# Values and output gate of the input projection as eight pairs of tiles with seven part products, x loaded tile by tile, key rotation on GpSimd

## The chip, the cores and the metric

The kernel runs on one core of one Trainium2 chip. The metric is the device time of one execution in microseconds (us), the lower the better. The core's engines are named as the profile names them: PE (TensorE: matmuls, with PEld for the loads of its stationary operand), DVE (VectorE), ACT (ScalarE), POOL (GpSimd) and SP (SyncE, whose queue issues the DMAs).

## The reference

The reference is one layer of a bidirectional encoder over 2048 rows of 1024 columns. Its first step is the subject here: an RMS norm and one large product, whose columns are cut up and go to different consumers.

```python
xn = rms_norm(h, ln_mix_g)
proj = xn @ w_in                      # 2512 columns: q, k, v, o of 512 each; 16 gates; 256 cq; 128 ckv; 64 kr
y_a = mlstm_group(q, k, v, o, gates + b_gates, conv_qk_w, conv_qk_b, mlstm_norm_g)
y_b = mla_group(cq, ckv, kr, q_norm_g, w_uq, kv_norm_g, w_ukv, cos, sin)
h = h + concat(y_a, y_b) @ w_out
h = h + conv_gated_mlp(rms_norm(h), ...)
h = h + sigmoid(rms_norm(h) @ w_ple_gate) * rms_norm(p @ w_ple_proj)
out = rms_norm(h)
```

`v` goes into the mLSTM as it is; `o` goes through a sigmoid and multiplies the mLSTM's normed output. `cq` and `ckv` are normed, `kr` is rotated by its position (`x1*cos - x2*sin`, `x2*cos + x1*sin`, 32 columns each).

## The kernel before

**Number format.** A float32 product is made from three matmuls in the PE's faster fp32r format: each operand is split into a rounded part and a remainder (`split`, lines 116 to 123: ACT casts at line 120, DVE subtracts at line 123), and `mm3` (lines 131 to 136) adds low x high, high x low and high x high. `split_g` (125 to 129) does the same for weights scaled by the norm's gain (ACT 128, DVE 129). The norm's inverse root is applied to the product's rows afterwards.

**The input projection, `in_proj` from line 176**, works in four stages. x comes already transposed, as eight k steps of 128 columns. One row tile is 128 of the 2048 rows; there are 16.

1. The "rest" columns (gates, cq, ckv, kr: 464). For each row tile `load_x` (221) loads x, `split_x` (242) puts its two parts into buffers that hold all of x from then on, and `nat` (212) runs 24 matmuls (8 k steps of 3). `ssq_x` (228 to 240) squares x on ACT, adds on DVE, sums over partitions with a matmul against ones (line 237), and takes the power -1/2 on POOL (240) into one column of `rcol`. The epilogue `rest` (248 to 276) adds the gate bias on DVE (252), copies the scaled product on ACT (255), takes the two norms' squares on ACT (261, 262) and their inverse roots on POOL (263, then `rsq`, 141 and 143), scales on DVE (265, 266), and rotates kr with six DVE instructions of 32 columns and a copy (269 to 275). `turn_rest` (278 to 284) transposes the 512 columns with four PE transposes (281), copies on ACT (283) and writes `rest_d`. The loop runs the epilogue two tiles behind the loads, the transposes two further behind.
2. The values: `load_w` loads and splits 512 columns of weights, `nat` makes the 16 tiles, DVE scales, and the result goes to `v_d`. Steps of the gate computation (`gates`, 631) are put between.
3. The output gate: the same, with a sigmoid on ACT and a multiplication by the norm's gain on DVE, to `o_d`.
4. q and k transposed, column tile by column tile (`block`, `conv`, lines 379 to 456), with x as the moving operand out of the buffers that hold all of it. Here `pump` (373) puts pieces of side work between the blocks (`absorb` at 518 and `q_up` at 563, products of the attention weights): a counter gains 0.986 a call and one piece runs for each whole unit. Here PE's order is fixed as written; in the stages before it a scheduler orders the instructions of each engine by data dependence and its own estimates.

After this come the mLSTM, the attention, the output projection and the feed-forward part (`stream`). The feed-forward part already computes pairs of row tiles with seven products in place of eight: `prep_a` (1367) and `prep_b` (1398) form the sums of a pair's x blocks and split them (through `up_pair`, 1350), and the weights' sums have the names of the table `OPX` (1167).

Eviction and accumulation use PSUM banks from four pools: four banks of the pool `sc` (`bank`), two of `tr` (`tbank`), one for the attention's products and one for small things (`pml`).

Of the kernel before, what the change touches and what calls it, by code (L numbers as in the profile page):

```python
# [36 lines left out]
LAG_T, LAG_X, LAG_R = 1, 2, 2  # L37
# [5 lines left out]
def pause(n):  # L43

    for _ in range(n):
        yield
# [14 lines left out]
class Block:  # L61
# [114 lines left out]
    def in_proj(self):  # L176
        nc, d = self.nc, self.d
        xh = [[self.at(f"x{4 * c + 2 * f}", [P, 4, 512], F32R, f"xh{c}{f}") for f in range(2)] for c in range(4)]
        xl = [[self.at(f"x{4 * c + 2 * f + 1}", [P, 4, 512], F32R, f"xl{c}{f}") for f in range(2)] for c in range(4)]
        wrot, rrot, trot, srot = _rot("w", (*range(9), 13)), _rot("w", range(9, 13)), _rot("t", range(4)), _rot("s", range(3))  # L180
        w_in = d["w_in"][0].rearrange("(a b p) c -> a p b c", b=2, p=P)

        def load_w(c0, n, before=None):

            out, raws = [], []

            def load(k2, parts=1):
                raw = self.at(next(rrot), [P, 2, 512], name="wraw")
                for i in range(parts):
                    bs = slice(2 * i // parts, 2 * (i + 1) // parts)  # L190
                    nc.sync.dma_start(raw[:, bs, :n], w_in[k2, :, bs, c0:c0 + n])
                raws.append(raw)
                return raw

            if before:
                load(0, 2)
                before(0)
                load(1, 2)
                before(1)
                load(2)  # L200
                load(3)
            for k2 in range(KT // 2):
                if k2 == len(raws):
                    load(k2)
                raw = raws[k2]
                for b in range(2):
                    w = self.at(next(wrot), [P, 2, 512], F32R, "wsp")
                    self.split_g(raw[:, b, :n], gcol[:, 2 * k2 + b:2 * k2 + b + 1], w[:, 0, :n], w[:, 1, :n])
                    out.append(w)
            return out  # L210

        def nat(st, ws, n):
            ps = self.bank()
            c, o = st // 4, (st % 4) * P
            for kt in range(KT):
                f, k = divmod(kt, 4)
                self.mm3(ps[:, :n], xh[c][f][:, k, o:o + P], xl[c][f][:, k, o:o + P],
                         ws[kt][:, 0, :n], ws[kt][:, 1, :n], kt == 0, kt == KT - 1)
            return ps

        def load_x(st):

            t = self.at(next(rrot) if st else "u2", [P, KT, P], name="x_t")
            if st:
                nc.sync.dma_start(t, d["x_turned"][:, :, st * P:(st + 1) * P])
            return t

        def ssq_x(st, x_t):

            sq = self.at("w13", [P, KT, P], name="x_sq")  # L230
            nc.scalar.activation(sq, x_t, AF.Square)
            ss = self.at("t7", [P, 4, P], name="x_ss")
            nc.vector.tensor_tensor(ss, sq[:, 0:4], sq[:, 4:8], op=ALU.add)
            nc.vector.tensor_tensor(ss[:, 0:2], ss[:, 0:2], ss[:, 2:4], op=ALU.add)
            ps = self.pml.tile([P, 4], F32, name="ssp", tag="ml")
            for i in range(2):
                nc.tensor.matmul(ps, ss[:, i], ones, start=i == 0, stop=i == 1)
            t = self.stat(1, "rsm")
            nc.vector.tensor_scalar(t, ps[:, 0:1], 1.0 / D, EPS, op0=ALU.mult, op1=ALU.add)
            nc.gpsimd.tensor_tensor(rcol[:, st:st + 1], t, self.nhalf[:, :1], op=ALU.pow)  # L240

        def split_x(st, x_t):
            c, o = st // 4, (st % 4) * P
            for f in range(2):
                self.split(x_t[:, 4 * f:4 * f + 4], xh[c][f][:, :, o:o + P], xl[c][f][:, :, o:o + P])


        def rest(st):
            ps = nat(st, ws, NREST)
# [8 lines left out]
            cos, sin, tt = sc[:, 0], sc[:, 1], sc[:, 2:6]  # L258
# [9 lines left out]
            x1, x2 = rs[:, 384:416], rs[:, 416:448]  # L268
            nc.vector.tensor_tensor(tt[:, 0, :], x1, cos, op=ALU.mult)
# [5 lines left out]
            nc.vector.tensor_copy(nn[:, 448:512], nn[:, 384:448])  # L275
# [11 lines left out]
        nc.sync.dma_start(gcol, d["g_turned"])  # L287
# [3 lines left out]
        nq, xq = {}, {}  # L291

        xq[0] = load_x(0)

        def first(f):

            fs = slice(4 * f, 4 * f + 4)
            if f < 2:
                nc.sync.dma_start(xq[0][:, fs], d["x_turned"][:, fs, 0:P])
                self.split(xq[0][:, fs], xh[0][f][:, :, 0:P], xl[0][f][:, :, 0:P])  # L300

        ws = load_w(OFF_R, NREST, first)
        for st in range(NT + LAG_X):
            if st + 1 < NT:
                xq[st + 1] = load_x(st + 1)
            if st == 0:
                gn = self.at("t5", [P, 384], name="gn")
                self.row_bcast(gn[:, 0:256], d["q_norm_g"][0], 256)
                self.row_bcast(gn[:, 256:384], d["kv_norm_g"][0], 128)
                bg = self.row_bcast(self.cst.tile([P, 16], F32, name="bg"), d["b_gates"][0], 16)  # L310
            if 1 <= st < NT:
                split_x(st, xq[st])
            if 0 <= st - 1 < NT:
                ssq_x(st - 1, xq.pop(st - 1))
            if 0 <= st - LAG_X < NT:
                nq[st - LAG_X] = rest(st - LAG_X)
            if 0 <= st - LAG_X - LAG_R < NT:
                turn_rest(st - LAG_X - LAG_R, nq.pop(st - LAG_X - LAG_R))

        nc.sync.dma_start(self.r_d.rearrange("(t p) -> p t", p=P), rcol)  # L320
        gates = self.gates()

        ws = load_w(OFF_V, 512)
        for st in range(NT):
            ps = nat(st, ws, 512)
            if st < LAG_R:
                turn_rest(NT - LAG_R + st, nq.pop(NT - LAG_R + st))
            t = self.at(next(trot), [P, 512], name="vo")
            nc.vector.tensor_scalar(t, ps, rcol[:, st:st + 1], None, op0=ALU.mult)
            nc.sync.dma_start(self.v_d[st], t)  # L330
            if st >= LAG_R:
                next(gates, None)
# [10 lines left out]
        for _ in gates:  # L343
            pass
# [1700 lines left out]
```

## Time and profile before

| what | us |
|---|---|
| median of 3 runs | 2892.84 (2892.28 to 2895.26) |
| the profiled execution | 2900.96 |
| its span on the core | 2899.2 |
| PE busy | 2853.5 |
| DVE busy | 2041.1 |
| ACT busy | 1524.4 |
| POOL busy | 158.0 |
| first matmul of the rest stage starts | 7.69 |
| first matmul of the values starts | 106.72 |
| values and output gate end | 283.92 |

A page of the profile gives an engine's busy time as a share of the span. Durations of single instructions overlap by their pipeline's length on PE, so a matmul's cost is read from the distance of starts, not from its own length. In a group's row, the number after the second bar is the idle time of that engine before the group and the instruction that ended it. A window's row gives busy time by engine (PE, PEld, DVE, ACT, POOL), then the granted PE clock as a share of full speed, the DMA share and GB/s.

### The profile page before, as it was taken

How to read it: one execution, taken by the hardware profiler on the slowest of the kernel's cores; microseconds unless marked ns; L12 is line 12 of the kernel's file. 1: busy time of each engine (PE TensorE's matmuls, PEld its weight loads, DVE VectorE, ACT ScalarE, POOL GpSimd, SP SyncE). 2: the span in 40 equal slices, each digit the busy share in tenths (PEclk: the TensorE clock that was granted, in tenths of full speed). 3: DMA queues.
4: the chain of work that ended last, by engine and by line, in shares of the span. 5: the costliest groups of instructions: out<-in, count | busy, mean ns of one | idle time of the engine just before them, and what ended most of it. 6: DMA issues, size and time to landing. Idle time of an engine off the chain costs nothing.

```text
span 2899.2 us, 40167 instructions
## 1 busy us (share of the span) xinstructions
PE 2853.5 (98%) x14110; PEld 2390.1 (82%) x14110; DVE 2041.1 (70%) x3790; ACT 1524.4 (53%) x3014; POOL 158.0 (5%) x295
## 2 busy tenths in 40 slices
PE   8999999999999999999999999999999999999998
PEld 7888888888888888788788888788888788888787
DVE  7521555777777777876677877767777867576787
ACT  7311544556666566765755555655555423254765
POOL 3100000000000010001000000000000000002111
PEclk9999999999999999999999999999999999999999
DMA  6612545653333333478834554657776757476865
GB/s 194 127 59 76 162 122 165 218 160 118 107 111 97 97 116 110 129 240 266 266 139 170 188 178 141 212 179 232 231 240 207 243 176 263 158 260 213 274 214 163
DMA packets 408314, 508.94 MB, mean 176 GB/s; under 512 B 34080, under 2 KB 271664, under 8 KB 408112
## 3 DMA queue, kind: packets, MB, share of 16 engines
q1 hardware_dynamic: 408112, 506.37, 55.3%
q8 instruction: 111, 1.82, 0.3%
q14 instruction: 91, 0.75, 0.1%
HBM read 324.16 MB, written 182.12 MB: 175 GB/s over the span
## 4 chain that ended last, share of the span: by engine, by line
PE 84%; DMA 5%; DVE 5%; ACT 3%; issue 3%; POOL 1%; SPq 0%; ACTq 0%; POOLq 0%; DVEq 0%
PE fy L1435 21%; PE fz L1435 14%; PE fx L1435 14%; PE bk L133 13%; PE ppv L989 3%; PE tb L977 3%; PE bk L914 2%; PE bk L916 2%; PE bk L915 2%; PE bk L918 2%; PE bk L917 2%; PE fs L133 2%; PE ppv L990 2%; PE gb L133 1%; PE mb L852 1%
## 5 line engine op out<-in xcount | busy, mean ns | idle before, releaser
L1435 PE MATMUL fz<-op,fw 128*128 128x512 f32 x1968 | 477.1, 391 | 2.7 <-ACT fw L120 2.7
L1435 PE MATMUL fy<-op,fw 128*128 128x512 f32 x1968 | 478.1, 391 | 1.6 <-ACT fy L1547 1.6
L1435 PE MATMUL fx<-op,fw 128*128 128x512 f32 x1968 | 476.0, 390 | 0.0
L1435 PEld LDWEIGHTS fy<-op,fw 128*128 128x128 f32 x1968 | 370.4, 189 | 79.4 <-ACT fy L1547 2.4
L1435 PEld LDWEIGHTS fz<-op,fw 128*128 128x128 f32 x1968 | 367.5, 188 | 79.5 <-ACT fw L120 3.6
L1435 PEld LDWEIGHTS fx<-op,fw 128*128 128x128 f32 x1968 | 368.0, 188 | 76.2 <-ACT fy L1547 0.2
L1435 PE MATMUL fy<-op,fwd 128*128 128x512 f32 (+1 forms) x984 | 239.8, 392 | 2.8 <-DVE uv L1420 2.6
L120 ACT CAST pt<-tb 128x512 fp32r<-128x512 f32 x256 | 147.2, 587 | 171.2 <-PE tb L977 170.4
L133 PE MATMUL bk<-wsp,xh 128*128 128x512 f32 (+1 forms) x768 | 234.1, 386 | 0.0
L1435 PEld LDWEIGHTS fy<-op,fwd 128*128 128x128 f32 x984 | 183.7, 189 | 41.7 <-DVE uv L1420 3.7
L919 DVE TENSOR_REDUCE mx<-bk 128x1 f32<-128x512 f32 x256 | 174.7, 684 | 40.5 <-PE bk L918 39.3
L123 DVE TENSOR_TENSOR pt<-tb,pt 128x512 fp32r<-128x512 f32 x256 | 174.1, 684 | 30.7 <-ACT pt L120 28.9
L937 ACT ACTIVATE pe<-bk,nm 128x512 f32<-128x512 f32 x256 | 174.8, 696 | 38.2 <-DVE nm L931 33.5
L989 PE MATMUL ppv<-pt,kv 128*128 128x512 f32 x512 | 188.6, 406 | 0.5 <-DVE pt L123 0.5
L133 PEld LDWEIGHTS bk<-wsp,xh 128*128 128x128 f32 x768 | 145.2, 189 | 25.1
L133 PE MATMUL bk<-wsp,xl 128*128 128x512 f32 (+1 forms) x384 | 150.7, 392 | 7.7 <-DVE xl L123 7.7
L133 PE MATMUL bk<-xh,wqk 128*128 128x512 f32 x480 | 157.1, 393 | 0.0
L977 PE MATMUL tb<-ident,pe 128*128 128x128 f32 x1024 | 150.3, 273 | 4.4 <-DVE pt L123 3.8
L990 PE MATMUL ppv<-pt,kv 128*128 128x256 f32 x512 | 144.7, 283 | 0.0
L977 PEld LDWEIGHTS tb<-ident,pe 128*128 128x128 f32 x1024 | 121.8, 140 | 25.0 <-DVE pt L123 6.8
L120 ACT CAST fw<-hraw 128x1024 fp32r<-128x1024 f32 (+1 forms) x72 | 70.2, 980 | 116.4 <-PE fx L1435 58.9
L123 DVE TENSOR_TENSOR fw<-fwr,fw 128x1024 fp32r<-128x1024 f32 x88 | 107.4, 1220 | 26.9 <-ACT fw L120 26.9
(363 smaller groups left out, 5113.5 us busy)
## 6 DMA issues: line engine op xcount, KB each, us to landing
fwr<-in_w_up SPq DMA_DIRECT2D x66, 512.0 KB, 5.2
fh<-h_d SPq DMA_DIRECT2D x48, 512.0 KB, 4.2
h_d<-fh SPq DMA_DIRECT2D x48, 512.0 KB, 4.0
s_d<-fwr SPq DMA_DIRECT2D x44, 512.0 KB, 3.3
fws<-s_d SPq DMA_DIRECT2D x44, 512.0 KB, 3.7
rw<-row_d SPq DMA_DIRECT2D x32, 512.0 KB, 5.5
tw_d<-tsum SPq DMA_DIRECT2D x60, 256.0 KB, 5.4
opr<-tw_d SPq DMA_DIRECT2D x60, 256.0 KB, 4.7
```

The lines of the kernel that those rows point to most:

```text
L120: nc.scalar.copy(hi, src)
L123: (sub or nc.vector).tensor_tensor(lo, src, _f(hi), op=ALU.subtract)
L133: mm = lambda *a, **k: self.nc.tensor.matmul(*a, **k, skip_group_check=more)
L914: mm(ps, ql, kh[:, ks], start=True, stop=False)
L915: mm(ps, qr, self.krl[:, ks], start=False, stop=False)
L916: mm(ps, qh, kl[:, ks], start=False, stop=False)
L919: nc.vector.tensor_reduce(s.mx[:, kb:kb + 1], ps, axis=AX.X, op=ALU.max)
L937: nc.scalar.activation(s.pe[:, kb % 2], s.banks[kb], AF.Exp, bias=s.nm, scale=ASCALE, accum_out=s.rs[:, kb:kb + 1])
L977: nc.tensor.transpose(t[:, j, :], s.p[kb][:, j * P:(j + 1) * P], self.ident)
L989: mm(w.ps, vh[:, ks], pts[kb][:, j], start=kt == 0, stop=False, skip_group_check=True)
L990: mm(w.ps[:, 0], vl[:, ks], pts[kb][:, j, 0], start=False, stop=kt == NT - 1, skip_group_check=True)
L1435: nc.tensor.matmul(out, a[:, k * P:(k + 1) * P], parts[lo][:, cols], start=first, stop=lo == 1 and k == last, skip_group_check=more)
```

## The change

The rest stage and the two stages after it are rewritten; lines of the new kernel are meant in this section.

- **First block.** The first four row tiles are made together, k step by k step, in four banks (`first_block`): each k step loads 512 rows of x and a piece of weights, splits both and runs 12 matmuls. Eight 128-column matmuls of the identity precede it. The sum of squares of the four tiles is formed along the way, and one instruction each makes four inverse norms.
- **x tile by tile.** Tiles 4 to 15 are loaded and split one at a time into buffers that are used again, and no copy of all x is kept. x is loaded again for the pairs (`load_pair`) and a third time for q and k (`load_qx`, 16 loads of 512 KB with 16 splits).
- **Key rotation on GpSimd.** The seven DVE instructions become five on GpSimd: two multiplications of 64 columns, a subtraction and an addition of 32, a copy of 64.
- **Values and gate in pairs.** With the values' weights as the left and the gate's as the right half of the columns, and the upper and lower half of the k steps, each pair of row tiles is a 2 x 2 block product made of seven products of 12 matmuls. The weight sums (`vo_sums`, `vo_late`) are made during the rest stage and the first pair, the sums of x by `prep_a` and `prep_b`. Two products of each pair (`rest_y`, `rest_z`) run in the next pair, those of the last pair in the q/k stage. Pairs 0 and 1 begin with one more matmul, which opens the bank that `nc.scalar.copy(s.y, x)` then fills.
- **Inverse norms.** `rcol` is turned by a PE transpose and written to `r_d` as 16 rows of 128, not element by element.
- **Around it.** The transposes of the last tiles move behind the pairs' preparation; the q/k stage's first column takes its four blocks in the order 0, 3, 1, 2; the side work's counter starts at -11 and gains 1.12 a call, and two pauses in `absorb` change (5 to 3; 2 to 3 for three of four heads).

The core of the diff:

```diff
+        def inv_rms(st, parts):
+            n = len(parts)
+            ps = self.pml.tile([P, n, 4], F32, name="ssp", tag="ml")
+            for i, ops in enumerate(parts):
+                for k, p in enumerate(ops):
+                    nc.tensor.matmul(ps[:, i], p, ones, start=k == 0, stop=k == len(ops) - 1)
+            t = self.stat(n, "rsm")
+            nc.vector.tensor_scalar(t, ps[:, :, 0], 1.0 / D, EPS, op0=ALU.mult, op1=ALU.add)
+            nc.gpsimd.tensor_tensor(rcol[:, st:st + n], t, self.nhalf[:, :n], op=ALU.pow)
...
+        def first_block():
...
+                self.split_g(raws[kt // 2][:, kt % 2, :NREST], gcol[:, kt:kt + 1], w[:, 0, :NREST], w[:, 1, :NREST])
+                self.split(xr[kt], x[:, 0], x[:, 1])
+                ws.append(w)
+                for n, (a, e) in enumerate(((0, 0), (1, 0), (0, 1))):
+                    for st in range(4):
+                        nc.tensor.matmul(ps[st][:, :NREST], x[:, a, st * P:(st + 1) * P], w[:, e, :NREST],
+                                         start=kt == 0 and n == 0, stop=kt == KT - 1 and n == 2)
+                if kt:
+                    sq = self.at(f"u{kt % 2}", [P, 512], name="x_q")
+                    nc.scalar.activation(sq, xr[kt], AF.Square)
+                    tt(acc, acc, sq, op=ALU.add)
...
-            nc.vector.tensor_tensor(tt[:, 0, :], x1, cos, op=ALU.mult)
-            nc.vector.tensor_tensor(tt[:, 1, :], x2, sin, op=ALU.mult)
-            nc.vector.tensor_tensor(tt[:, 2, :], x2, cos, op=ALU.mult)
-            nc.vector.tensor_tensor(tt[:, 3, :], x1, sin, op=ALU.mult)
-            nc.vector.tensor_tensor(nn[:, 384:416], tt[:, 0, :], tt[:, 1, :], op=ALU.subtract)
-            nc.vector.tensor_tensor(nn[:, 416:448], tt[:, 2, :], tt[:, 3, :], op=ALU.add)
-            nc.vector.tensor_copy(nn[:, 448:512], nn[:, 384:448])
+            turn, x12 = nc.gpsimd.tensor_tensor, rs[:, 384:448].rearrange("p (a c) -> p a c", a=2)
+            for a in range(2):
+                turn(sc[:, 2 + 2 * a:4 + 2 * a], x12, sc[:, a:a + 1].broadcast_to([P, 2, 32]), op=ALU.mult)
+            turn(nn[:, 384:416], sc[:, 2], sc[:, 5], op=ALU.subtract)
+            turn(nn[:, 416:448], sc[:, 3], sc[:, 4], op=ALU.add)
+            nc.gpsimd.tensor_copy(nn[:, 448:512], nn[:, 384:448])
...
+        def vo_sums():
+            for k in range(4):
+                r0, r1, r2, r3 = [vraw[k][:, i] for i in range(4)]
+                g1, g2 = gcol[:, k:k + 1], gcol[:, k + 4:k + 5]
+                nc.scalar.activation(r0, r0, AF.Copy, scale=g1)
+                self.split(r0, *vo_place("B11", k))
+                yield
+                stt(r1, r1, g1, r0, op0=ALU.mult, op1=ALU.subtract)
+                self.split(r1, *vo_place("T1", k))
+                yield
+                stt(r1, r3, g2, r1, op0=ALU.mult, op1=ALU.subtract)
+                self.split(r1, *vo_place("T2", k))
+                yield
+                tt(r0, r1, r0, op=ALU.subtract)
+                yield
...
+        for st in range(4, NT):
+            if st + 2 < NT:
+                load_x(st + 2)
+            if st in (5, 7, 9, 11):
+                vo_load(st // 2 - 2)
+            if st == 12:
+                load_pair(0)
+            if st > 4:
+                done[st] = nat(st)
+            ssq_x(st, xq.pop(st))
+            if st + 2 < NT:
+                split_x(st + 2, xq[st + 2])
+            for i in ((0, 1), (2,), (3,), (4,), (5,))[st - 4] if st < 9 else (st - 3,):
+                finish(i)
+            for _ in range(2 * (st > 6)):
+                next(sums, None)
+            if st == 14:
+                prep = chain(self.prep_a(VO), self.prep_b(VO))
+            if st > 13:
+                for _ in range(2):
+                    next(late)
+                    next(prep)
...
+        for p in range(NT // 2):
+            s = Pair()
+            s.p, s.ops = p, self.ops.pop(VO + p)
+            x, s.y = [self.bank(name=f"vo{n}") for n in "xy"]
+            s.z = self.tbank([P, 512], name="voz")
+            if p < 2:
+                nc.tensor.matmul(s.y, s.ops["A11"][0][:, 0:P], vo["B11"][0][0], start=True, stop=True)
+            prod(x, s.ops["A11"], "B11")
+            nc.scalar.copy(s.y, x)
...
+            prod(s.z, s.ops["S1"], "T1")
+            s.p5 = self.at(("t3", "t2")[p % 2], [P, SB], name="p5")
+            nc.scalar.copy(s.p5, s.z)
...
+            if prev:
+                rest_y(prev)
+            prod(s.y, s.ops["S2"], "T2", True)
+            s.c12 = self.at(("t0", "t1")[p % 2], [P, SB], name="c12")
+            nc.scalar.copy(s.c12, s.y)
...
+                self.up_prep(VO + p + 1)
+            if 0 < p < last - 1:
+                load_pair(p + 2)
...
+            prod(x, s.ops["A12"], "B21", True)
+            values(2 * p, x)
+            if prev:
+                rest_z(prev)
...
+            prod(s.y, s.ops["S3"], "T3", True)
+            tt(s.p5, s.p5, s.y, op=ALU.add)
+            opens(2 * p + 1, s.p5)
...
-        due = [0.0]
+        due, made = [-11.0], set()
...
-            due[0] += 0.986
+            due[0] += 1.12
```

More of the change, by code (lines that the diff above doesn't have):

```diff
@@ L181, in in_proj @@
         w_in = d["w_in"][0].rearrange("(a b p) c -> a p b c", b=2, p=P)
[L183 to L210, printed above, removed]
@@ L347, in in_proj @@
+        for _ in chain(sums, prep):
+            pass
+        pr = self.pml.tile([NT, P], F32, name="rrp", tag="ml")
+        nc.tensor.transpose(pr, rcol, self.ident)
+        rr = self.at(next(srot), [NT, P], name="rr")
+        nc.vector.tensor_copy(rr, pr)
+        nc.sync.dma_start(self.r_d.rearrange("(t p) -> t p", p=P), rr)
+        for st in range(NT - 3, NT + 2):
+            finish(st)
+        load_pair(1)
+        cw = self.at(next(srot), [32, P], name="cw")
         nc.sync.dma_start(cw[0:24], d["conv_qk_w"][0].rearrange("t (j p) -> (t j) p", p=P))
```

276 lines of the change are left out of this document (191 added, 85 removed).

## The prediction

> **What bounds the kernel now.** I read the page's busy shares first, then the chain that ended last by line, then busy times cut into the stages of the input projection, then that chain inside the first 130 us.
>
> ```profile
> PE 2853.5 (98%) x14110; PEld 2390.1 (82%) x14110; DVE 2041.1 (70%) x3790; ACT 1524.4 (53%) x3014; POOL 158.0 (5%) x295
> PE fy L1435 21%; PE fz L1435 14%; PE fx L1435 14%; PE bk L133 13%; PE ppv L989 3%; PE tb L977 3%; PE bk L914 2%; PE bk L916 2%; PE bk L915 2%; PE bk L918 2%; PE bk L917 2%; PE fs L133 2%; PE ppv L990 2%; PE gb L133 1%; PE mb L852 1%
> ...
> 7.69:106.72 99.03, 97.05 (x504) 85.77 (x505) 70.40 (x257) 67.55 (x149) 36.08 (x61) 1.00 0.69 166
> 106.72:283.92 177.20, 176.93 (x791) 145.85 (x790) 47.80 (x124) 24.45 (x48) 1.14 (x3) 1.00 0.24 75
> ...
> 20.00:40.00 20.00, 19.17 (x103) 16.73 (x102) 15.97 (x62) 16.76 (x39) 9.66 (x16) 1.00 0.59 168
> 40.00:60.00 20.00, 19.27 (x107) 17.21 (x105) 16.20 (x59) 13.76 (x30) 9.69 (x13) 1.00 0.56 159
> 80.00:100.00 20.00, 20.00 (x108) 18.03 (x107) 10.73 (x51) 8.96 (x25) 7.22 (x16) 1.00 0.61 139
> ```
>
> The windows give span, then busy time and count of PE, PE's weight load, DVE, ACT and POOL, then the granted clock, the DMA share and GB/s. TensorE bounds the kernel (98%), and the matmuls of line 133, which the change thins out, are 13% of the end's chain. The first window holds the "rest" columns of the projection, the second the values and the output gate. In the second PE is busy 176.93 of 177.20 us while DVE and ACT are little used: a matmul taken out there is time taken out, as long as the helpers keep up. In the first, DVE and ACT are at 16 to 17 of 20 us at the beginning, and PE is not wholly fed.
>
> ```profile
> 7.69 7.12 PE bk L133 x24
> 16.65 0.95 POOL rcol L240
> 22.50 0.74 POOL rsr L143
> 42.70 5.14 PE bk L133 x24
> 47.84 0.44 PE rtp L281 x4
> 48.28 0.34 PE ssp L237 x4
> 48.62 5.12 PE bk L133 x24
> 119.26 10.91 PE bk L133 x48
> ```
>
> These pieces of the chain (start, duration, what) say more: up to 42.70 us the chain runs through the tile's epilogue (inverse norm on POOL, ACT, DVE), after it through PE alone. A rest tile then costs 0.44+0.34+5.12 = 5.90 us, and a matmul of the values or gate 10.91/48 = 0.2273 us.
>
> **The products saved.** Values and gate are 2 x 16 tiles x 24 = 768 matmuls of 512 columns now. Eight pairs of tiles with seven products of 12 are 672. Two more are there only to set a bank's start (pairs 0 and 1). Saved: 96 x 0.2273 = 21.8 us; added: 2 x 0.2273 = 0.45 us.
>
> **The first block.** Four tiles are now made k by k, so that PE can begin with one eighth of x and w.
>
> ```profile
> 1.17 3.08 DMA wraw<-in_w_in
> 4.32 1.28 ACT L128
> 5.62 0.69 ACT wsp L128
> ...
> 9.02 0.59 PE L133 MATMUL bk<-wsp,xl 128*128 128x464 f32 x1
> 10.18 0.59 PE L133 MATMUL bk<-wsp,xl 128*128 128x464 f32 x1
> ```
>
> The first weights landed at 4.3 us, ACT then spent 1.28 us on a table and 0.69 on the split. The new kernel issues them no later and takes the table load earlier, so PE can start at about 5.25 us (5.0 to 7.69). At first three matmuls take 10.18-9.02 = 1.16 us against 3 x 5.12/24 = 0.64 later; over the first 3.6 us that loses 1.7 us, as it does now. 96 matmuls x 0.2133 + 1.7 = 22.2, to 27.4 us.
>
> ```profile
> L123 DVE TENSOR_TENSOR xl<-x_t,xh 128x512 fp32r<-128x512 f32 x31 | 20.5, 684 | 0.8 <-ACT xh L120 0.8
> L129 DVE SCALAR_TENSOR_TENSOR wsp<-wraw,gcol,wsp 128x464 fp32r<-128x464 f32 (+1 forms) x12 | 8.1, 715 | 0.0
> ```
>
> Per k DVE has 0.715 for w, 0.684 for x and as much for the squares, 2.1 us, and ACT some 1.9, against PE's 12 x 0.2133 = 2.56: they keep up. Tiles 4 and 5 with the sums of squares between follow (2 x 5.12 + 2 x 0.34), to 38.4 us.
>
> **The first stall.** On PE's queue the transposes of tile 0's epilogue stand ahead of tile 6. On ACT and on DVE that epilogue stands behind the first three of four k steps of the new weight sums (lines 318 to 329): on ACT down to the scaling of the fourth raw block, which must have landed. The loads ahead of it are 4.0 MB of first block, 2 MB of x tiles and about 4 MB of raw values and gate weights.
>
> ```profile
> DMA packets 8190, 5.28 MB, mean 264 GB/s; under 512 B 868, under 2 KB 8190, under 8 KB 8190
> ```
>
> That is DMA over the first 20 us. About 10 MB at 264 to 290 GB/s end at 35 to 38 us. Tile 0's inverse norm then comes at about 39.5, ACT's scaled copy at 40.5, two tiles of rotation on POOL (next part) and 1.4 us of its query and key norms by 46, DVE's row at 47.2, and tile 6 starts at 47.7. PE so waits 9.3 us. The ten tiles 6 to 15 at 5.90, and a last 0.44, end at 107.2; half of a second slow start (0.9) makes 108.1. Today the values start at 106.72: **1.4 us lost**, since what the early start gains goes into the stall. Queued behind the stall on PE is everything; on ACT and DVE only the later tiles' epilogues, which have slack. Between the last bounds: a stall of nothing gives -9, one of 14 us gives +5. Three transposed tiles (3 x 0.44 = 1.3 us) move from the rest stage into the pairs: their x 0.44 is counted there, **1.3 us**.
>
> **Rotation on GpSimd.** Per tile seven DVE instructions go, five on POOL come.
>
> ```profile
> L269 DVE TENSOR_TENSOR sc<-rs,sc 128x32 f32<-128x32 f32 x15 | 2.8, 189 | 1.9 <-ACT rs L255 1.9
> L275 DVE COPY nn<-nn 128x64 f32<-128x64 f32 x15 | 2.9, 192 | 0.2
> L240 POOL TENSOR_TENSOR rcol<-rsm,nhalf 128x1 f32<-128x1 f32 x16 | 15.4, 964 | 43.9 <-DVE rsm L239 43.9
> L263 POOL TENSOR_SCALAR ssq<-ssq 128x1 f32<-128x1 f32 x15 | 5.6, 375 | 21.6 <-ACT nn L262 21.6
> L141 POOL TENSOR_SCALAR rsm<-ssq 128x2 f32<-128x2 f32 x15 | 3.6, 242 | 1.2
> L143 POOL TENSOR_TENSOR rsr<-rsm,nhalf 128x2 f32<-128x2 f32 x15 | 11.4, 761 | 1.3
> ...
> L1948 POOL TENSOR_TENSOR rsr<-pse,psm 128x1 f32<-128x1 f32 x1 | 0.2, 191 | 0.1
> masks.py:199 POOL TENSOR_SCALAR_AFFINE_SELECT ident<-ident 128x128 f32<-128x128 f32 x1 | 0.3, 294 | 0.1
> L829 POOL TENSOR_SCALAR_AFFINE_SELECT mk<-rw 128x512 f32<-128x512 f32 x32 | 25.9, 834 | 874.0 <-DVE qi L834 535.6 <-PE mb L852 188.7 <-DVE mx L919 105.8
> ```
>
> DVE loses at most 7 x 0.19 = 1.3 us a tile, and no wait of PE ends on that. POOL's multiplication of 64 columns is in no row. From below: 0.191 us, that of one column. From above: (834-294)/384 = 1.41 ns a column with one input, 2.8 with two, so 0.191 + 64 x 2.8 = 0.37 us. With 0.37, 0.37, 0.28, 0.28, 0.28 and gaps of 0.05 a tile's rotation is 1.85 us. With the norms (0.375+0.242+0.761 = 1.4) and the inverse norm (0.55 undisturbed, below) POOL has 3.8 us in a tile's 5.90, and it fits. But POOL is slower beside DVE:
>
> ```profile
> L240 POOL TENSOR_TENSOR rcol<-rsm,nhalf x16: 548/922/1557, 16.7 to 96.2; 128x1 f32<-128x1 f32 x16
> ...
> 44.44 1.30 POOL L263 TENSOR_SCALAR ssq<-ssq 128x1 f32<-128x1 f32 x1 [0.53 <-ACT nn L262]
> 44.97 0.68 DVE L123 TENSOR_TENSOR xl<-x_t,xh 128x512 fp32r<-128x512 f32 x1
> ```
>
> One operation took 548 to 1557 ns, and a step of one column that has a mean of 375 ns took 1.30 us and ended with a run of two-input DVE instructions (44.97+0.68). If each of five rotation steps waits 0.3 us, POOL is at 5.3; at 0.56 it is at 6.6, 0.7 over a tile's period for a dozen tiles, 8 us. I take **1.9 us**, near the lower end, since DVE is idle a fifth of the time at 40 to 60 us and nearly half at 80 to 100. The Trainium skill, "SBUF — State Buffer", section "Who interferes with whom", says that DVE instructions with two SBUF inputs and GpSimd instructions that read SBUF take a shared port pair by turns, each for its whole length; the 1.30 us agrees. By that rule the sum would be that of the second rival.
>
> **The pair stage.** Per pair PE has 7 x 12 x 0.2273 = 19.1 us. DVE's share: splits of x sums and operands, four evictions, two additions.
>
> ```profile
> L123 DVE TENSOR_TENSOR fw<-fwr,fw 128x1024 fp32r<-128x1024 f32 x88 | 107.4, 1220 | 26.9 <-ACT fw L120 26.9
> L120 ACT CAST xh<-x_t 128x512 fp32r<-128x512 f32 x31 | 18.1, 615 | 5.9 <-DMA x_t<-in_x_turned 5.9
> ```
>
> Four splits of 128x1024 (4 x 1.22), sums of as much, and evictions of 0.64 come to some 11 us, with gates (47.80-us window, mostly unchanged) 18 at most; ACT is at about 7. Covered by PE's 19.1. The two pairs at the beginning are tighter: the last sums, the splits of the late operands, and the epilogues of three tiles make 36 us of DVE beside 38 of PE. At the end 16 splits of x for the q/k stage (18.7 us of DVE, 16 of ACT) and 8.4 MB of reload have some 45 us of PE: covered at 190 GB/s. I cost all of this at nothing; without the cover the price is a DVE excess of 0 to 8 us. SP issues 37 more transfers; a reload that waits there for its buffer holds the epilogue's writes behind it, which nothing reads before the q/k stage. The side work there is the same, paced anew, and the small inverse-norm write (16 rows instead of single elements) is off the path: nothing.
>
> **Sum.** -21.8 + 0.45 + 1.4 + 1.3 + 1.9 = -16.8 us. The profiled execution took 2900.96 us (span 2899.2), 8.1 above the median 2892.84; as every term is a difference, I take it from the median: **2876.0 us**.
>
> **Rivals.**
> 1. *The stall is shorter.* If loads come faster (slices of the first 20 us reach 400 GB/s) or the epilogue is issued before the sums, tile 6 starts 9 us earlier and POOL keeps up: -16.8 - 9 - 1.9, about 2865. For it: PE begins 2.4 us earlier and x comes in eighths. Against: the queue order of ACT.
> 2. *POOL becomes the bound of the rest stage* (slower). If each of POOL's reads waits for a DVE instruction or two (0.9 us each, as in the 1.30 us row), five steps add 4.6 us to 3.8: 8.4 us a tile against 5.90, 2.5 x 12 tiles = 30 us: -16.8 + 30, about 2906. It decides from the point where POOL passes 5.90 us a tile, and takes back all the gain at 7.3. Against: those gaps of DVE.
> 3. *The pairs do not run at PE's pace.* The change then doesn't do what it says: a bank freed late by DVE or ACT idles PE between products. A full 2.73 us (one product) per pair is the whole gain, giving 2893 to 2898; half the pairs, or the first two's DVE excess of 8 us, gives 2884. Against: 8 pairs with two banks in work at a time and copies of 0.6 us behind products of 2.7.
>
> **How the numbers follow.** Forecast (2870 to 2887): 0.50. Rival 1: 0.16. Rival 2: 0.12. Rival 3: 0.22, half of it still faster. 0.2%, or 5.8 us, is about what a measurement of this kernel can tell from no change. Faster: 0.50+0.16+0.11 = 0.77. Within: 0.10. Slower: 0.13. The range leaves out the end of rival 1 and rival 2's long stall: 2862 to 2897.
>
> **What would show it.** 672 matmuls of 512 columns at 0.227 us in the pairs, PE starting near 5.3 us, a PE hole of about 9 us near 38 to 48 us with POOL in the chain, pairs starting near 108 us, and POOL's multiplication of 64 columns with a mean under 0.6 us. I am wrong if that hole is absent or repeats tile by tile, if the multiplication's mean is about 1.2 us, or if PE idles between products. By the Trainium skill, "TensorE: Matmul & The Clock Gate", Part 1, an idle time of some 3.4 us halves PE's clock until it has been busy as long again; the slow first matmuls above agree, and it would show as a second set of 0.39 us matmuls after the hole, 1.7 us where I took 0.9.

## The result, and the profile after

| | us |
|---|---|
| before, median of 6 runs | 2896.04 (2892.28 to 2900.03) |
| after, median of 6 runs | 2905.01 (2901.67 to 2907.27) |
| profiled execution of after | 2901.67, span 2899.9 |

After to before is 1.0026, 95% interval 1.0016 to 1.0036: 7.5 us slower by this ratio, 9.0 by the medians, where 16.8 us faster was forecast. (The forecast's 2876.0 us was counted from 2892.84, the median of the first three runs of before; that of six is 3.2 us higher.) The change does what it says, and the time went elsewhere. The chain that ended last by engine from the page of before, then busy time and the same chain from the page of after:

```profile
PE 84%; DMA 5%; DVE 5%; ACT 3%; issue 3%; POOL 1%; SPq 0%; ACTq 0%; POOLq 0%; DVEq 0%
...
PE 2839.6 (98%) x14025; PEld 2376.9 (82%) x14025; DVE 2129.2 (73%) x3787; ACT 1592.2 (55%) x3099; POOL 194.8 (7%) x372
PE 79%; DMA 6%; DVE 5%; ACT 4%; issue 3%; POOL 2%; SPq 0%; POOLq 0%; ACTq 0%; DVEq 0%
```

PE has 13.9 us less to do (2853.5 before) and its share of the chain fell from 84% to 79%: PE now waits. The two profiled executions have nearly the same span, because that of before was a long one for its kernel (2900.96 against a median of 2896.04) and that of after the shortest of its six; so the traces are compared by landmarks. The windows say where, three of before and then those of after (span, then PE, PEld, DVE, ACT, POOL busy, clock, DMA share, GB/s):

```profile
31.00:47.00 16.00, 15.27 (x82) 13.29 (x81) 12.57 (x48) 12.28 (x29) 9.03 (x13) 1.00 0.70 195
47.00:107.00 60.00, 60.00 (x326) 54.17 (x325) 39.00 (x156) 36.21 (x86) 20.95 (x39) 1.00 0.64 133
107.00:140.00 33.00, 32.73 (x149) 26.69 (x148) 14.13 (x43) 4.94 (x14) 1.14 (x3) 1.00 0.57 151
...
7.00:31.00 24.00, 24.00 (x121) 21.49 (x119) 19.48 (x31) 18.03 (x30) 0.00 (x0) 1.00 0.92 309
31.00:47.00 16.00, 9.50 (x42) 8.17 (x42) 12.02 (x31) 11.16 (x23) 7.17 (x19) 0.79 0.72 229
47.00:107.00 60.00, 54.72 (x281) 47.52 (x280) 42.48 (x91) 39.49 (x86) 47.01 (x88) 0.97 0.40 111
107.00:140.00 33.00, 22.88 (x100) 17.72 (x100) 20.74 (x42) 17.05 (x40) 19.50 (x36) 0.82 0.56 159
140.00:268.00 128.00, 128.00 (x566) 105.11 (x566) 86.65 (x156) 55.88 (x77) 0.00 (x0) 0.99 0.38 123
```

The pairs themselves (last row) are as forecast: PE is busy all of the time. PE lacks 6.5 us at 31 to 47, 5.3 in the rest stage's steady part, and 10.1 at the opening of the pairs, where POOL is still at work. Pieces of PE's timeline show what ended those waits (start, duration, and in brackets the idle time before and its releaser), and how the matmuls behind them ran:

```profile
4.83 20.46 PE L244 MATMUL bk<-wsp,xb 128*128 128x464 f32 x96
38.21 1.01 PE L200 MATMUL ssp<-ones,x_ss 128*128 128x4 f32 x4 [6.37 <-DVE rsm L202]
39.09 6.19 PE L133 MATMUL tb<-wsp,xs 128*128 128x464 f32 x21
46.20 5.27 PE L133 MATMUL bk<-wsp,xs 128*128 128x464 f32 x24
72.66 0.58 PE L200 MATMUL ssp<-ones,x_ss 128*128 128x4 f32 x4 [1.43 <-DVE gt L257]
73.78 6.58 PE L133 MATMUL bk<-wsp,xs 128*128 128x464 f32 x24
107.52 5.37 PE L133 MATMUL bk<-wsp,xs 128*128 128x464 f32 x24
119.84 0.38 PE L411 MATMUL rrp<-ident,rcol 128*16 128x128 f32 x1 [4.43 <-POOL rcol L203]
136.51 0.47 PE L283 MATMUL rtp<-ident,nn 128*128 128x128 f32 x1 [4.59 <-POOL nn L277]
136.64 3.33 PE L435 MATMUL voy<-op,fw 128*128 128x512 f32 x7
320.78 1.43 PE L133 MATMUL gb<-woa,uvs 128*128 128x512 f32 x5 [0.77 <-DVE woa L123]
```

Tile 6 starts at 46.20 and tile 15 at 107.52: (107.52-46.20)/9 = 6.81 us a tile, where before had 5.90.

The waits cost more than their length. Behind each of the four longest (6.37, 1.43, 4.43 and 4.59 us) PE ran at half pace for some microseconds. The granted clock of 0.50 shows it in these windows, and from 119 to 122 us behind the wait of 4.43:

```profile
38.00:40.00 2.00, 1.79 (x6) 1.68 (x7) 1.23 (x7) 1.10 (x2) 1.76 (x2) 0.50 1.08 348
74.00:76.00 2.00, 2.00 (x7) 1.72 (x7) 0.87 (x3) 0.03 (x1) 0.93 (x3) 0.50 0.81 211
137.00:140.00 3.00, 3.00 (x8) 2.32 (x8) 1.29 (x2) 1.62 (x3) 0.00 (x0) 0.50 0.37 102
```

The 21 matmuls from 39.09 take 6.19 us where 24 take 5.27 at 46.20, and the 24 at 73.78 take 6.58. Busy time times the missing share of the clock gives an estimate of 2.1 us lost behind the wait of 6.37, 1.6 behind that of 1.43 and 2.4 behind that of 4.59. In before the clock is 1.00 in all of these windows.

The chain of after in the rest stage (47 to 107 us) is mostly POOL's: its lines in this row make 65%. One tile's pieces of it follow:

```profile
by line: POOL sc L274 18.7%; issue 11.4%; POOL nn L277 10.4%; POOL rcol L203 10.0%; POOL rsr L143 9.8%; POOL ssq L267 6.5%; POOL nn L276 6.0%; DMA sc<-in_rope 5.4%; POOL nn L275 3.5%; ACT rs L260 3.3%; DVE nn L270 3.2%; DMA vv_d<-nn 3.1%; P
...
83.93 1.38 POOL sc L274 x2
85.33 0.99 POOL rcol L203
87.09 1.12 POOL nn L277
88.77 0.74 POOL rsr L143
```

The wait at 136.51 shows why POOL is late. Its one multiplication of 64 columns stands beside this run of DVE:

```profile
130.45 4.89 POOL L274 TENSOR_TENSOR sc<-rs,sc 128x64 f32<-128x64 f32 x1 [2.08 <-DVE vt L344]
...
130.34 0.68 DVE L1595 TENSOR_TENSOR xr<-xr 128x512 f32<-128x512 f32 x1
130.94 0.68 DVE L123 TENSOR_TENSOR op<-vr,op 128x512 fp32r<-128x512 f32 x1
131.54 1.22 DVE L123 TENSOR_TENSOR fw<-xr,fw 128x1024 fp32r<-128x1024 f32 x1
132.68 0.68 DVE L1596 TENSOR_TENSOR xr<-xr 128x512 f32<-128x512 f32 x1
133.28 0.68 DVE L123 TENSOR_TENSOR op<-vr,op 128x512 fp32r<-128x512 f32 x1
133.88 1.28 DVE L123 TENSOR_TENSOR op<-vt,op 128x512 fp32r<-128x512 f32 x2
```

DVE's two-input instructions follow each other without a gap, and POOL's multiplication ends (135.34) when the last of them does (135.16). Undisturbed it takes 0.32 us (below).

### The profile page after: what moved, and what is told of

Same layout as the page of the kernel before. It is cut to its first block, busy times and chain, and to the rows that moved or that the text cites. A ratio compares the mean times of both kernels' runs of the same rounds, so it can differ in the third digit from the quotient of the medians.

```text
span 2899.9 us, 40259 instructions
## 1 busy us (share of the span) xinstructions
PE 2839.6 (98%) x14025; PEld 2376.9 (82%) x14025; DVE 2129.2 (73%) x3787; ACT 1592.2 (55%) x3099; POOL 194.8 (7%) x372
## 4 chain that ended last, share of the span: by engine, by line
PE 79%; DMA 6%; DVE 5%; ACT 4%; issue 3%; POOL 2%; SPq 0%; POOLq 0%; ACTq 0%; DVEq 0%
PE fy L1622 21%; PE fz L1622 14%; PE fx L1622 14%; PE bk L133 4%; PE ppv L1176 3%; PE tb L1164 3%; PE voy L435 2%; PE bk L1101 2%; PE bk L1102 2%; PE bk L1103 2%; PE bk L1104 2%; PE bk L1105 2%; PE ppv L1177 1%; PE fs L133 1%; PE vox L435 1%
## 5 line engine op out<-in xcount | busy, mean ns | idle before, releaser
L1622 PEld LDWEIGHTS fy<-op,fwd 128*128 128x128 f32 x984 | 182.7, 188 | 41.1 <-DVE uv L1607 3.2
L120 ACT CAST op<-opr 128x512 fp32r<-128x512 f32 x165 | 96.2, 621 | 56.9 <-PE fy L1622 15.4
L1670 DVE SCALAR_TENSOR_TENSOR fgv<-uv,fcw,fgv 128x1024 f32<-128x1024 f32 x88 | 112.8, 1282 | 15.4 <-ACT fgv L1668 14.6
L123 DVE TENSOR_TENSOR op<-opr,op 128x512 fp32r<-128x512 f32 x165 | 107.1, 685 | 20.8 <-ACT op L120 20.2
```

The source lines that it names most:

```text
L120: nc.scalar.copy(hi, src)
L123: (sub or nc.vector).tensor_tensor(lo, src, _f(hi), op=ALU.subtract)
L1622: nc.tensor.matmul(out, a[:, k * P:(k + 1) * P], parts[lo][:, cols], start=first, stop=lo == 1 and k == last, skip_group_check=more)
L1670: nc.vector.scalar_tensor_tensor(t, u[:, tap:tap + 2 * SB], self.taps[:, tap, ct:ct + 1], t, op0=ALU.mult, op1=ALU.add)
```

## The experiments

Theory A: GpSimd's rotation is the loss, since its steps wait for DVE's two-input instructions and stand in the tile's path. Theory B: the weight sums that DVE and ACT now do ahead of the epilogues are the loss, wherever the rotation runs. All ratios are to the kernel before, run again beside each batch, with 95% intervals; 0.0010 is 2.9 us. After itself is 1.0026. One more kernel, probe, ran once, and only its trace is used.

| kernel | ratio | interval |
|---|---|---|
| rope_dve | 0.9982 | 0.9973 to 0.9991 |
| three_rs | 1.0016 | 1.0007 to 1.0025 |
| before_rope_pool | 1.0016 | 1.0007 to 1.0025 |
| no_hoist | 1.0137 | 1.0123 to 1.0150 |
| last_three_dve | 1.0000 | 0.9991 to 1.0008 |
| pace_only | 1.0004 | 0.9995 to 1.0012 |
| late_rrp | 0.9977 | 0.9966 to 0.9987 |
| old_pace | 0.9965 | 0.9953 to 0.9976 |
| late_sums | 1.0002 | 0.9993 to 1.0011 |
| five_dve | 0.9959 | 0.9946 to 0.9972 |
| five_dve_rrp | 0.9953 | 0.9941 to 0.9965 |
| dve_plus_reads | 1.0038 | 1.0026 to 1.0050 |
| dve_plus_memset | 1.0002 | 0.9993 to 1.0011 |
| half_late | 0.9952 | 0.9940 to 0.9964 |

### The rotation: rope_dve, before_rope_pool, last_three_dve

```diff
-            turn, x12 = nc.gpsimd.tensor_tensor, rs[:, 384:448].rearrange("p (a c) -> p a c", a=2)
...
-            nc.gpsimd.tensor_copy(nn[:, 448:512], nn[:, 384:448])
+            cos, sin, tt6 = sc[:, 0], sc[:, 1], sc[:, 2:6]
+            x1, x2 = rs[:, 384:416], rs[:, 416:448]
+            nc.vector.tensor_tensor(tt6[:, 0, :], x1, cos, op=ALU.mult)
...
```

> The changed kernel with the key rotation back on DVE (its seven instructions), all else kept. Theory A (GpSimd's steps are stretched by runs of two-input DVE instructions, and set the tile's period): tiles 7 to 15 come about 6.0 us apart in place of 6.7, the wait of 4.6 us in the first pair goes, and the time is 10 to 20 us below the changed kernel's 2905, about 2890. Theory B (the new weight sums on DVE and ACT ahead of the epilogue are the loss, wherever the rotation runs): less than 4 us below.

It is 12.7 us faster than after (1.0026 to 0.9982), as theory A said, and faster than before. PE's timeline of rope_dve, tiles 6 and 15:

```profile
46.40 5.27 PE L133 MATMUL bk<-wsp,xs 128*128 128x464 f32 x24
...
101.28 5.26 PE L133 MATMUL bk<-wsp,xs 128*128 128x464 f32 x24
```

Nine tiles take 54.88 us, 6.10 each, 6.4 us less than in after. From tile 15 to the first q/k matmul (268.1 here, 281.1 in after) another 6.8 go. The wait that ends at 38 us is about as long (6.76 us against 6.37), so theory B's place is untouched by the edit. That GpSimd's reads hold up DVE is a small part at most: at 47 to 107 us DVE's splits of 128x1024 take 1240 ns on average in after and 1216 in rope_dve. The window of the pairs' opening in rope_dve (columns as above):

```profile
107.00:140.00 33.00, 27.12 (x123) 21.92 (x123) 27.02 (x67) 21.18 (x42) 7.53 (x12) 0.90 0.62 179
```

PE still lacks 5.9 us in it, most of it in one wait of 5.50 us for the last tile's inverse norm, behind which the clock is again 0.50 (113 to 116 us). DVE is busy 27.02 of 33.

before_rope_pool is the kernel before with only this edit the other way (seven DVE instructions replaced by the five on GpSimd).

> The kernel before with only the rotation moved to GpSimd. Theory A: the period of a rest tile rises from 5.90 to 6.3 to 6.8 us, and the time rises by 5 to 15 us to about 2905. Theory B: within 3 us of the kernel before.

It loses 4.6 us, just under theory A's range: without the new work on DVE the rotation costs a third of what it costs in after. The longer period that theory A named did not come: from 43 us on the tiles stay 5.90 us apart but for two, of 7.40 and 6.49. last_three_dve takes DVE for `st >= NT - 3` and GpSimd for the others.

> The changed kernel with the rotation of tiles 13 to 15 on DVE and of the others on GpSimd. It parts the loss into its two places. If the wait in the first pair (one multiplication of 4.89 us beside an unbroken run of DVE) is a third of it: 4 to 6 us below 2905, with the tiles 6.7 us apart as before. If the tiles' period is all of it: within 2 us.

7.5 us come from three tiles alone. The period stays (48.48 to 109.96, 6.83 us a tile), and the wait of 4.6 us in the first pair is gone. So a good half of the rotation's price lies in the tail, where DVE's run has no gap. It is more than the 4 to 6 us expected, because with the wait of 4.59 us its half pace goes too: 4.6 + 2.4 = 7.0.

### What in it costs: probe, dve_plus_reads, dve_plus_memset, three_rs

probe puts this ahead of the kernel before, four times: with no `op`, with a one-input DVE instruction, with a two-input one, and with a copy on ACT, of 128x512 each:

```diff
+                for i in range(16):
+                    op(i)
+                for i in range(10):
+                    nc.gpsimd.tensor_tensor(po[:, i], pa[:, 0, :64], pc, op=ALU.mult)
```

> The kernel before with a measurement ahead of it that adds nothing to the result: ten multiplications of 128x64 on GpSimd, first alone, then beside 16 one-input DVE instructions of 128x512, then beside 16 two-input ones, then beside 16 copies on ACT. Theory A: about 0.3 us each alone, beside one-input DVE and beside ACT; beside two-input DVE each takes 0.6 us or more, or the ten end only after the DVE run. If operand size alone makes them slow: the same in all four.

POOL's timeline of probe, ten multiplications each, beside one-input DVE, two-input DVE and ACT:

```profile
11.84 4.63 POOL L196 TENSOR_TENSOR pro<-pr,prc 128x64 f32<-128x64 f32 x10 [0.55 <-ACT prc L192]
18.45 7.00 POOL L196 TENSOR_TENSOR pro<-pr,prc 128x64 f32<-128x64 f32 x10 [1.99 <-ACT prc L192]
29.38 4.83 POOL L196 TENSOR_TENSOR pro<-pr,prc 128x64 f32<-128x64 f32 x10 [3.92 <-ACT prc L192]
```

These are 0.46, 0.70 and 0.48 us each. The ten "alone" and the first half of those beside ACT fell beside the kernel's own DVE work, so they show nothing undisturbed. Three others fell beside a nearly idle DVE and do; the first row has them, and the next two have DVE's two-input instructions with POOL beside them and without:

```profile
10.43 0.87 POOL L196 TENSOR_TENSOR pro<-pr,prc 128x64 f32<-128x64 f32 x3
...
L187 DVE TENSOR_TENSOR pr<-pr,pr 128x512 f32<-128x512 f32 x11 | 7.9, 790 | 0.0
L187 DVE TENSOR_TENSOR pr<-pr,pr 128x512 f32<-128x512 f32 x5 | 3.1, 679 | 0.0
```

From 0.29 us the multiplication grows to 0.46 beside one-input DVE, which theory A did not expect, and to 0.70 beside two-input DVE. There it does not wait for the end of DVE's run: POOL found a turn for each DVE instruction, which took 790 ns meanwhile and 679 when POOL was done. In the tail of after, POOL found no turn in seven instructions. A gap between DVE's instructions does not part the two cases: left alone they start 0.60 us apart in both (at 25.93, 26.53 and 27.13 us in probe). What does is not shown. The Trainium skill, "SBUF — State Buffer", "Who interferes with whom", says that a two-input DVE instruction and a GpSimd read contend for a port pair that is an exclusive lock. The row of 0.70 us agrees; that a whole run of DVE shuts POOL out is shown by the 4.89 us alone.

The next two leave the rotation on DVE and add work on GpSimd whose results nothing uses, dve_plus_reads the first five instructions a tile, dve_plus_memset the other five.

```diff
+            turn = nc.gpsimd.tensor_tensor
+            for _ in range(2):
+                turn(sc[:, 6:8], sc[:, 2:4], sc[:, 4:6], op=ALU.mult)
+            for _ in range(2):
+                turn(sc[:, 6], sc[:, 2], sc[:, 5], op=ALU.subtract)
+            nc.gpsimd.tensor_copy(sc[:, 6:8], sc[:, 2:4])
...
+            for _ in range(5):
+                nc.gpsimd.memset(sc[:, 2:8], 0.0)
```

> rope_dve with five more GpSimd instructions a tile that nothing uses, of the kinds and sizes of the rotation (two of 64 columns with two inputs, two of 32, a copy of 64), reading DVE's products. If GpSimd's reads beside DVE, or GpSimd's longer queue ahead of the inverse norms, make the loss: back up by 4 to 10 us over rope_dve (ratio to the kernel before about 1.000). If the loss came only from the rotation's own result arriving late: within 2 us of rope_dve.

> rope_dve with five memsets of 192 columns a tile on GpSimd at the same places, as long as the rotation undisturbed (about 1.3 us) but reading nothing from SBUF. If reading beside DVE is the loss (theory A): within 2 us of rope_dve and 3 us or more below dve_plus_reads. If the mere length of GpSimd's queue is: the same as dve_plus_reads.

Neither theory's number came alone: over rope_dve the memsets cost 5.8 us, where theory A had under 2, and the reads 16.2, where 4 to 10 were expected (each with some 4 us of noise). Groups of POOL at 38 to 125 us, of dve_plus_reads and then of dve_plus_memset:

```profile
L283 POOL TENSOR_TENSOR sc<-sc 128x64 f32<-128x64 f32 x26 | 15.4, 593 | 14.2 <-DVE sc L277 10.4 <-DVE rsm L202 2.7
```

```profile
L282 POOL MEMSET sc<- 128x192 f32 x75 | 19.1, 257 | 7.2 <-DVE nn L279 4.6
L203 POOL TENSOR_TENSOR rcol<-rsm,nhalf 128x1 f32<-128x1 f32 x12 | 14.4, 1198 | 21.5 <-DVE rsm L202 21.4
```

A memset keeps its 0.26 us beside DVE, a read of 64 columns grows from 0.32 to 0.59. So roughly a third of the price of the reads is there without reading, from five more instructions in GpSimd's queue ahead of the next inverse norm. The rest comes with reading: the longer instructions, and the waits for DVE's products (10.4 us in the first row); these two are not parted. The rotation's result arriving late isn't needed for it. Undisturbed durations come from no_hoist, where DVE is idle half of the time (busy 41.17 of the 87 us); first its groups, then those of after, same window:

```profile
L274 POOL TENSOR_TENSOR sc<-rs,sc 128x64 f32<-128x64 f32 x18 | 5.4, 322 | 7.2 <-ACT rs L260 6.6 <-DMA x_t<-in_x_turned 0.7
L277 POOL COPY nn<-nn 128x64 f32<-128x64 f32 x9 | 2.1, 236 | 0.6
```

```profile
L274 POOL TENSOR_TENSOR sc<-rs,sc 128x64 f32<-128x64 f32 x30 | 18.5, 636 | 14.4 <-ACT rs L260 14.4
L277 POOL COPY nn<-nn 128x64 f32<-128x64 f32 x15 | 9.2, 612 | 1.0
```

three_rs (`("t0", "t1", "t6")[st % 3]` for the buffer of the scaled tile) tests whether two buffers close a ring.

> The changed kernel with three buffers for the scaled rest tile in place of two. Theory A with a ring (the scaled copy of tile n+2 waits for DVE's last read of tile n, which waits for GpSimd's inverse root of tile n, which stands behind the rotation of tile n+1): the tile's period falls from 6.7 to 5.9 to 6.2 us, 5 to 8 us off, about 2898. If GpSimd's own work is the bound, or theory B holds: within 2 us of 2905.

A miss: 2.9 us, with intervals that overlap. POOL's idle time on ACT's scaled copy fell from 14.4 us to 0.7, so that ring was there, but 10.0 us of waiting for DVE's first step of the inverse norm (0.3 in after) came in its place. Tiles 6 to 15 still came at 47.33 to 107.35, 6.67 us apart, so the third buffer does not open the loop that sets the period.

### The sums: no_hoist, late_sums, half_late

no_hoist puts the loop over tiles 4 to 15 under `manual_schedule(engines={ET.DVE, ET.Activation})`.

> The changed kernel with ACT and DVE in the order of the program text through tiles 4 to 15, so that the weight sums come behind the epilogues of tiles 0 to 3. Theory B: PE's wait of 7 us at 31 us goes below 2, and the time falls by 5 to 10 us. Theory A: the wait moves, GpSimd keeps the tile's period at 6.5 us or more, and the time is within 3 us of 2905 or above it.

32 us slower than after. PE's wait at 31 us is gone, but DVE and ACT, in the text's order, wait for POOL inside each tile, and tiles come about 10 us apart. It shows the cost of that order, not of the sums. late_sums leaves the order free and gives the sums one more condition:

```diff
+        stt(gcol, rcol[:, 0:1].broadcast_to([P, KT]), 0.0, gcol, op0=ALU.mult, op1=ALU.add)
```

> late_rrp with the weight sums made to wait for the first inverse norm (the gain column is rewritten as itself plus zero times that norm), so that they follow the epilogues of tiles 0 and 1. Theory B in its smaller form: PE's wait of 6.8 us at 32 us goes to 2 or less, and the time is 4 to 7 us below late_rrp, if the sums still get done before the pairs. If they then come late: pair 0 waits for its operands and the gain is below 2 us or a loss.

PE's timeline of late_sums:

```profile
38.51 5.28 PE L133 MATMUL bk<-wsp,xs 128*128 128x464 f32 x24
...
100.26 5.29 PE L133 MATMUL bk<-wsp,xs 128*128 128x464 f32 x24
```

Tile 6 starts 7.7 us sooner than in after (38.51), and tile 15 at 100.26: 6.86 us a tile. What was won at 32 us was lost again. Tile 6 starts 9.3 us ahead of late_rrp's (47.82) and tile 15 only 2.7 (102.97 there), although the rotation is on DVE in both; from tile 15 to the first q/k matmul this run then takes 275.1-100.26 = 174.8 us, late_rrp 268.1-102.97 = 165.1. The longest waits of PE ahead of the pairs (3.08 us on ACT's scaled copy, 2.32 on DVE's gate bias) are for the last epilogues. In all it is 7.3 us slower than late_rrp. half_late does it for two of four k steps, on top of five_dve_rrp.

> five_dve_rrp with the weight sums of only the last two of four k steps made to wait for the first inverse norm. If the hoisted sums of all four were too many at once and those of late_sums too late, PE's first wait falls from 7 to about 3 to 4 us without slower tiles behind it: 2 to 4 us below five_dve_rrp. If DVE's work in the rest stage is full, what is saved at 32 us comes back tile by tile: within 1.5 us.

No difference from five_dve_rrp (0.9952 against 0.9953). PE's first wait stayed at 7.54 us, since DVE's first step of the norms still stood behind the other two steps, so this run doesn't part order from work. late_sums does: the first wait comes from the sums standing ahead of the norms, and goes when they stand behind.

### The rest: late_rrp, pace_only, old_pace, five_dve, five_dve_rrp

late_rrp is rope_dve with the transpose of `rcol` and its write moved to the start of pair 2.

> rope_dve with one thing moved: the transpose of the inverse norms on PE and its write stand in pair 2 in place of ahead of pair 0. If PE's queue order makes the 5.5 us wait of the first pair (the transpose needs the last tile's inverse norm), 3 to 5.5 us go, to about 2889. If the pair would wait anyway for its own operands or for the transposes of tiles 13 to 15: less than 2 us.

Nothing (1.5 us, intervals overlap): PE then waits for ACT's copies of the last epilogues at the same place (2.27 and 1.50 us). pace_only and old_pace take the pace of the side work back, on after and on rope_dve:

```diff
-            due[0] += 1.12
+            due[0] += 0.986
...
-        yield from pause(3)
+        yield from pause(5)
...
-            yield from pause(3 if h else 2)
+            yield from pause(2)
```

> The changed kernel, rotation still on GpSimd, with the side work of the q/k stage at its former pace (0.986, pauses of 5 and 2). If the pace is a loss of its own beside the rotation: 3 to 5 us below 2905, and the gaps at 318 to 330 us gone. If it only helped after the rotation had gone back to DVE: within 2 us of 2905.

> rope_dve with the side work of the q/k stage at its former pace (0.986 a call, pauses of 5 and 2) and still begun at -11. If the pace brings the products of absorb ahead of their weights, the gaps of 4.3 us at 308 to 320 us go and the time falls by 3 to 5 us, unless the work then left over at the end costs as much. If the loads are late through the three-fold reading of x, the gaps stay and the time is within 2 us of rope_dve.

6.4 and 4.9 us. The q/k matmuls of before, after and pace_only (count, durations, first and last start):

```profile
L133 PE MATMUL bk<-xh,wqk x480: 387/389/507, 283.9 to 494.3; 128*128 128x512 f32 x160
```

```profile
L133 PE MATMUL bk<-xh,wqk x480: 387/389/476, 281.1 to 500.9; 128*128 128x512 f32 x160
```

```profile
L133 PE MATMUL bk<-xh,wqk x480: 388/389/476, 282.7 to 498.8; 128*128 128x512 f32 x160
```

Before takes 210.4 us; after 219.8, of which 5.4 are the two products put there: 4.0 us lost; pace_only 216.1, 0.3 lost. The waits of after on `woa` there (1.06, 0.77, 0.85 and 0.76 us) are gone in pace_only. five_dve is old_pace with GpSimd's five instructions issued on DVE, five_dve_rrp adds late_rrp's move.

> old_pace with the rotation on DVE in the five instructions written for GpSimd instead of seven. The rest stage is held up by DVE's work beside the sums, so 2 instructions less a tile are worth 0.1 to 0.2 us each tile where DVE is late: 0 to 2 us below old_pace, 2887 to 2889.

> five_dve with the transpose of the inverse norms moved to pair 2. As late_rrp moved nothing, within 2 us of five_dve; if the two together free the first pair, 2 to 4 us below.

1.7 us each, inside the intervals. five_dve_rrp is 13.6 us faster than before and, with half_late, the fastest here.

## Why the prediction was wrong, point by point

- **The products saved: right.** 672 matmuls at 2.72 us a dozen (pairs at 140 to 268 us, PE busy 128.00 of 128.00).
- **The first block: right in kind.** Start 4.83 instead of 5.25, and 20.46 us for 96 matmuls instead of 22.2: the loss of 1.7 us at half pace did not come. The likely reason is the eight small matmuls ahead (1.34 to 5.09 us), to which the forecast gave no effect; no run leaves them out.
- **The first stall: nearly right.** The inverse norms do stand behind the weight sums on DVE, but the first PE instruction to wait for them was the next tile's sum of squares, one step earlier in PE's queue than forecast: 6.37 us in place of 9.3. The half pace behind it cost some 2 us, where 0.9 was taken. Tile 6 came at 46.20 in place of 47.7. With the rotation out of the way (rope_dve) tile 15 starts at 101.28, in before at 101.25: the early start and the stall cancel, where 1.4 us lost were forecast.
- **Rotation on GpSimd: the step that failed.** "I take 1.9 us, near the lower end" measured 12.7 us (rope_dve). There are two errors in it. The DVE work beside which GpSimd reads was taken from the kernel before, although the change adds the sums and makes the splits of x longer (128x1024 in 1.24 us, where before had 128x512 in 0.68); the copy that takes 0.24 us undisturbed took 1.12 at 87.09, beside one of them. before_rope_pool, with the old DVE work, costs 4.6. And the price was asked tile by tile against a period of 5.90 us that POOL's busy time never reaches (47.01 us in 60, or 5.3 a tile of 6.81), while POOL lies in series with DVE and ACT in each tile; a step that is not full can still set the period. The sign that was to tell, a mean of POOL's multiplication under 0.6 us or about 1.2, came out at 0.636 and did not tell.
- **The second rival** named POOL, and its 2906 us lies next to the measured time by luck. Its 30 us were all to come from the rotation, at 8.4 us a tile; that gave 12.7, and the rest came from the two points below. It was to decide only with POOL above 5.90 us a tile.
- **The pairs' opening: at nothing, measured 9.6 us.** From tile 15 to the first q/k matmul before takes 283.9-101.25 = 182.7, rope_dve 268.1-101.28 = 166.8, and 5.4 more stand in the q/k stage: 10.4 saved of 21.3. 1.3 was forecast for the moved transposes, so 9.6 are left, where the bound given was 8. Most of them fall in the opening: PE idles 5.9 us there, and half pace behind the wait of 5.50 us costs an estimated 2.4 more. DVE is busy 27.02 of the 33 us from 107 to 140 us in rope_dve, so the cover of "36 us of DVE beside 38 of PE" left little room for waits between engines.
- **The side work "the same, paced anew": at nothing, measured 4.0 us** in the q/k stage and 6.4 in all (pace_only). Its products came ahead of their loads: the gap of 0.77 us above is one of four.
- **The clock.** The forecast gave half pace 0.9 us, once. In after it came four times by 140 us, once behind a wait of only 1.43 us, where the rule that the prediction quotes asks for some 3.4; the measurement decides. The terms measured above contain it.
- **The sum by what was measured**: -21.3 + 12.7 + 9.6 + 1.3 + 4.0 = +6.3; the 9.6 is what was left over in its stretch, so the sum closes in part by construction. From the end of the q/k matmuls to the first of the mLSTM's products on line 852 (1039 in after) another 1.3 are lost (500.9 to 679.5 against 494.3 to 671.6), which makes 7.6. The last of these products start at 1188.1 and 1179.8, 8.3 apart; the ratio gives 7.5 and the medians 9.0.

What stays open: how the 9.6 us of the pairs' opening part between the epilogues and the operands (late_rrp shows only that the transpose of the norms is not it), and why POOL gets a turn beside one run of DVE and none beside another.

## What to carry to other kernels

Moving small reads to GpSimd is priced by what DVE will be doing beside them after the change, not before it: a run of two-input DVE instructions can hold a GpSimd read back until it ends, and beside each single one it loses a turn. Ask of an added in-order step not only whether its engine has room, but whether it stands in a loop through other engines; there its length, and what it waits for, can set the loop's period while the engine is still idle part of the time. Count a wait of PE by more than its length: the granted clock was 0.50 for some microseconds behind each of the four longest in after. Work taken out of PE is won only as far as the helpers' new work fits elsewhere: move it (late_sums) and see whether the wait goes or only changes its place.

## What the runs showed of the hardware that was not expected

One GpSimd multiplication of 128x64 took 4.89 us beside a run of seven two-input DVE instructions in after, 0.70 beside another such run in probe, 0.46 beside one-input DVE and 0.29 undisturbed; memsets on GpSimd kept their 0.26 us beside DVE. A wait of PE of 1.43 us already had a clock of 0.50 behind it (74 to 76 us in after), while one of 2.58 us in dve_plus_reads (67.76) had 1.00, so the length alone does not decide. With sixteen small passes on PE from 1.34 us, while the first loads were on their way, no half-pace start was seen: 96 matmuls in 20.46 us, 0.213 each.
